# The state space layer's token pieces, tap matrices and value half in a new order

## The chip, the cores and the metric

The kernel runs on one core of one Trainium2 chip. Its time is the device time of one execution in microseconds (us); less is better. The times shown here are of three executions, and of one more that the hardware profiler recorded.

The core has five engines that run side by side and wait for each other through semaphores: PE (TensorE, matrix products), DVE (VectorE), ACT (ScalarE), POOL (GpSimd) and SP (SyncE, which here does nothing but issue transfers). In a profile PEld is the loading of PE's stationary operand. SP, ACT and POOL each have a queue of transfers, shown as SPq, ACTq and POOLq. Each engine takes its instructions in a fixed order, and issuing a transfer is one of them: an engine that has to wait before it may issue does nothing else meanwhile.

## The reference

A trunk of four residual layers on 256 tokens of 1024 channels. Each layer has a token mixer, cross-attention to 256 memory tokens, and a gated MLP. The mixer of layer 2 is a state space layer (S5), and only this layer is changed:

```python
def s5_mixer(h, a_re, a_im, log_dt, b_re, b_im, c_re, c_im, d, w_glu):
    ...                                     # a_bar, b_bar, c_mat: complex, 64 groups of 16 channels, 64 states each
    def chunk_step(state, u_blk):
        bu = jnp.einsum('bcgi,gpi->bcgp', u_blk.astype(jnp.complex64), b_bar)
        a_seq = jnp.broadcast_to(a_bar, bu.shape)
        _, xs = lax.associative_scan(_lin_rec_combine, (a_seq, bu), axis=1)
        xs = xs + a_pow[None] * state[:, None]
        y = jnp.real(jnp.einsum('bcgp,gip->bcgi', xs, c_mat))
        return xs[:, -1], y
    ...
    y = ys.transpose(1, 0, 2, 3, 4).reshape(B, S, D) + d.astype(f32) * u
    y = jax.nn.gelu(y).astype(h.dtype)
    val, gate = jnp.split(y @ w_glu, 2, axis=-1)
    return val * jax.nn.sigmoid(gate)
```

The input `h` of the mixer is the residual stream after an RMS norm. After the mixer the same layer computes the cross-attention, whose keys and values come from the memory tokens alone: `kv = mem_n @ wkv`.

## The kernel before

All weights are fp32. A weight tile of 1 MB is loaded into one of three buffers of the pool `raw`, split into a high and a low part (`whi` by ACT at line 70, `wlo` by DVE or POOL at line 71), and each product is three matmuls (`mm3`, lines 65 to 67). The pool `acts` has two buffers for each of the tags `ah` and `al`, `big` has one (`xs`), and `kv` holds single tiles (`vh`, `vl` and others).

**The state space layer** works on blocks of 8 tokens, 32 of them. Inside a block the output is a product with a matrix of taps; across blocks 64 x 64 complex states are carried. The matrices were made in the layers before and lie in DRAM: `blD` (B, four tiles of 1 MB, `bl`), `tD` (taps, four tiles `tu`) and `caD` (C times powers, four tiles `ou`). In the order of the program the layer does this:

- `rstd` and the scaled tokens `u`, for two halves `tt` of 128 tokens. Each half is written in two column halves, one by DVE and one by ACT (line 962).
- Eight transfers from `u` to `uc` (line 968), 128 KB each, SBUF to SBUF: for each `tt` and each quarter `q` of the channels, 128 pieces of 1 KB go to 16 partitions, those from `32 * q + 16 * tt` on. Quarters 0 and 1 are issued by SP, 2 and 3 by ACT.
- `db`, the product of the skip gain D and the norm's gain, broadcast to 128 partitions by eight small transfers (line 980); POOL multiplies them and then makes the table `tab8` of powers.
- `ur`, a copy of `uc` in another order (line 994, ACT and DVE by turns), transposed by PE into `v` (line 998), then the products with the four `bl` tiles, giving S (line 1012), S transposed into `SX` (lines 1027 and 1029), and the scan, 44 DVE instructions (lines 1049 to 1066) that give the states X. The scan keeps two PSUM banks, `sc` and `two`.
- The products of `v` with the four tap tiles `tu` into the accumulators (line 1078), then of X with the four `ou` tiles (`carry`, line 1098), gelu (lines 1107 and 1109), transposes of the result (line 1115, split at lines 1118 and 1119) and the GLU product with `w_glu`, eight tiles of 1 MB.

**Work between these steps.** PE would idle in this chain, so units of the keys and values of the cross-attention are put at named points by `fill`: `k1 k2` at "u", `k3` at "s" after the products with `bl`, `v0` (the values' first half) at "scan0" and `v1` (the second half) at "scan1". The values' weights `v0`, `v1` are split by POOL.

**What sets the order.** A scheduler orders the instructions of each engine at build time by its own estimates; `behind(x)` makes the following ones come after x in it. A tile's buffer is given to the next tile when the last reader is done, and the transfer that fills it waits for that. The transfers of SP and ACT use eight completion semaphores by turns (DMAHW0 to DMAHW7); a transfer is not issued before the one eight earlier, which had the same semaphore, has landed. The fourth transfer on ACT's queue shares its semaphore with the `bl` tile that SP issues at 814.03 us:

```order
L968 DMA uc_8468<-u_8467 16x8x256 [waits DMAHW2_49,PE_49,Activation_49]
L968 DMA uc_8468<-u_8467 16x8x256 [waits DMAHW4_49]
L968 DMA uc_8468<-u_8467 16x8x256 [waits DMAHW6_49,Activation_49]
L968 DMA uc_8468<-u_8467 16x8x256 [waits DMAHW0_49]
L70 CAST kh_6196<-mm_8516 128x512 [waits PE_49]
```

These are rows of ACT's order before; the last one is the first cast that stands behind the four transfers on ACT.

Of the kernel before, what the change touches and what calls it, by code (L numbers as in the profile page):

```python
# [8 lines left out]
F32 = mybir.dt.float32  # L9
# [5 lines left out]
P = 128  # L15
# [21 lines left out]
class Trunk:  # L37
# [901 lines left out]
    def s5_mixer(self, l, sp):  # L939
        nc, a = self.nc, self.a  # L940
        bls = []

        def land(mm):
            pool, tag = ((self.kv, "vh"), (self.kv, "vl"), (sp, "X"), (self.raw, "raw"))[mm]
            bl = pool.tile([P, 2, 4, 2, 2, 64], F32, tag=tag, name="bl")
            nc.sync.dma_start(bl[:].rearrange("p m q x r k -> p m (q x r k)"), self.blD[:, 2 * mm : 2 * mm + 2, :])
            bls.append(bl)

        land(0)
        land(1)  # L950
        rs = []
        for tt in range(TT):
            rs.append(self.rstd(self.ss[tt]))
        self.fill("u0")
        u = self.big.tile([P, TT, D], F32, tag="xs", name="u")
        uc = sp.tile([P, 8, 16, 16], F32, name="uc")
        chain, firsts, last = [], [None, None], None
        for tt in range(TT):
            r = rs[tt]
            for nh, f in enumerate((nc.vector.tensor_scalar_mul, nc.scalar.mul)):  # L960
                s = slice(512 * nh, 512 * (nh + 1))
                done = f(u[:, tt, s], self.h[:, tt, s], r[:, 0:1])
                firsts = firsts[1:] + [done.ins]

                for q in (2 * nh, 2 * nh + 1):
                    at = 32 * q + 16 * tt
                    queue = nc.scalar if nh else nc.sync
                    moved = queue.dma_start(  # L968
                        uc[at : at + 16].rearrange("c t a j -> c t (a j)"), u[:, tt, 256 * q : 256 * (q + 1)]
                    )  # L970
                    last = last if nh else moved
        chain.append(done.ins)

        chain.append(self.scaled)
        with self.behind(last.ins):
            land(2)
        db = sp.tile([P, 2, 256], F32, name="db")
        for i, row in enumerate((a["s5_d"][0], a["mix_norm_g"][l])):
            for q in range(4):
                nc.sync.dma_start(db[32 * q : 32 * q + 32, i, :], row[256 * q : 256 * (q + 1)].partition_broadcast(32))  # L980
        with self.behind(self.powed):
            nc.gpsimd.tensor_mul(db[:, 0, :], db[:, 0, :], db[:, 1, :])
            tab8 = self.s5_eighths(sp)
# [3 lines left out]
        self.after = [chain, chain + [last.ins]]  # L987
        self.fill("u1")
        self.late = ()
        v = self.acts.tile([P, 16, P], F32, tag="ah", name="v")  # L990
        ev = [nc.scalar.copy, nc.vector.tensor_copy]
        ur = self.acts.tile([P, 16, 8, 16], F32, tag="ah", name="ur")
        for b in range(4):
            ev[b % 2](ur[:, 4 * b : 4 * b + 4], uc[:, ::-1, 4 * b : 4 * b + 4, :].rearrange("p t a j -> p a t j"))
        for b in range(4):
# [8 lines left out]
        for mm in range(4):  # L1004
# [10 lines left out]
                        )  # L1015
            ev[mm % 2](S[:, 2 * mm : 2 * mm + 2].rearrange("p a x b -> p (a x b)"), ps[:])
        self.fill("s")

        SX = self.acts.tile([P, NCH, 2, GP], F32, tag="al", name="SX")
        sv = SX[:].rearrange("p c x (q m) -> p m x q c", m=8)  # L1020
        for b in range(4):
            ps = self.bank()
            for m2 in range(2):
                m = 2 * b + m2
# [3 lines left out]
            for m2 in range(2):  # L1028
                last = ev[1 - m2](sv[:, 2 * b + m2], ps[:, 256 * m2 : 256 * (m2 + 1)].rearrange("p (x q c) -> p x q c", x=2, q=4))
# [36 lines left out]
                steps.append(vec.tensor_add(new, new, pr).ins)  # L1066
        self.late = steps[7:8]
        self.fill("scan0")
        values = self.multiplied

        Y = self.accs()
        for mm in range(4):
            tu = self.raw.tile([P, 2, 2, 4, P], F32, tag="raw", name="tu")
            landed = nc.sync.dma_start(tu[:].rearrange("p r m q k -> p r (m q) k"), self.tD[mm]).ins
            with self.behind(values):
                for m, par, q in [(m, par, q) for m in (2 * mm, 2 * mm + 1) for par in range(2) for q in range(4)]:
                    c0 = (m % 4) * P
                    nc.tensor.matmul(
                        Y[2 * par + m // 4][32 * q : 32 * q + 32, c0 : c0 + P], v[:, 2 * m + par, 32 * q : 32 * q + 32], tu[:, par, m % 2, q, :],
                        start=m % 4 == 0, stop=False, tile_position=(0, 32 * q), skip_group_check=True,  # L1080
                    )
        self.late = steps[-1:]
        self.fill("scan1")
        self.late = ()

        def carry(mm):
            pool, tag = ((self.big, "xs"), (self.acts, "ah"), (self.raw, "raw"), (self.raw, "raw"))[mm]
            ou = pool.tile([P, 2, 4, 2, P], F32, tag=tag, name="ou")
            with self.behind(landed):
                nc.sync.dma_start(ou[:].rearrange("p m q x k -> p m (q x) k"), self.caD[:, 2 * mm : 2 * mm + 2])  # L1090
            for m2 in range(2):
                m = 2 * mm + m2
                for x in range(2):
                    for q in range(4):
                        for par in range(2):
                            rows = slice(64 * par, 64 * par + 64)
                            c0 = (m % 4) * P
                            done = nc.tensor.matmul(
                                Y[2 * par + m // 4][32 * q : 32 * q + 32, c0 : c0 + P], X[rows, x, 8 * q + m, :], ou[rows, m2, q, x, :],
                                start=False, stop=x == 1, tile_position=(64 * par, 32 * q), skip_group_check=True,  # L1100
                            )
            return done.ins
# [8 lines left out]
        def turn(h, yh):  # L1111
# [8 lines left out]
            return last  # L1120

        carry(0)
        carry(1)
        y0, g0 = gelu(0)
        yT = self.act_pair()
        carry(2)
        done = carry(3)
        with self.behind(done):
# [3 lines left out]
        for nh in range(2):  # L1132
            acc = self.accs() if nh else [self.bank() for _ in range(4)]
            for kh in range(2):
                for gate in (1, 0):
# [3 lines left out]
                    for tt in range(TT):  # L1139
                        for k in range(4):  # L1140
                            c = 2 * k + kh
# [5 lines left out]
            for tt in range(TT):  # L1147
# [4 lines left out]
                last = vec.tensor_add(hs, hs, sg)  # L1152
# [271 lines left out]
```

## Time and profile before

| | us |
|---|---|
| median of three executions | 1514.38 |
| lowest and highest | 1512.39, 1520.98 |
| profiled execution, its own time | 1520.19 |
| span from its first to its last instruction | 1518.5 |
| PE busy | 1440.2 (95% of the span) |
| mean granted TensorE clock | 0.974 |

The profiled execution is near the upper end of the three. 1.7 us lie around its span. In rows of the trace times are in us from the start of the span, `out<-in` names the tiles that an instruction writes and reads, and the bracket at a row's end says how long the engine idled before it and what ended that. The layer's mixer lies between 810 and 950 us.

### The profile page before, as it was taken

The page shows a single profiled execution, that of the slowest core. Times are in us where ns is not written, and L with a number is a line of the kernel's source. Part 1 is how long each engine was busy: PE and PEld are TensorE (multiplying, and loading weights), DVE is VectorE, ACT ScalarE, POOL GpSimd, SP SyncE. Part 2 cuts the span into 40 slices and gives each one's busy share as a digit, 9 for nine tenths or more (in the row PEclk, how much of TensorE's full clock was granted, in tenths as well). Part 3 has the DMA queues.
Part 4 walks back from the last instruction along what each step waited for, and adds up shares of the span by engine and source line. Part 5 has one row for each costly group of instructions (what it writes and reads, how often), then busy time and mean ns, then how long its engine had stood idle before and what let it go on. Part 6 is the DMA issues. An engine that isn't in the chain of part 4 may idle for free.

```text
span 1518.5 us, 25333 instructions
## 1 busy us (share of the span) xinstructions
PE 1440.2 (95%) x10318; PEld 1324.3 (87%) x10318; DVE 1096.0 (72%) x1720; ACT 833.4 (55%) x1338; POOL 139.6 (9%) x148
## 2 busy tenths in 40 slices
PE   7999998899899999999997779999999999999997
PEld 7898997798898998999986667989999999899996
DVE  6868677678787666998874755768777686677775
ACT  6554543465677455655544334656555575465553
POOL 3401000000000000011113420000000030000000
PEclk9999999999899999999998889999999999999999
DMA  7567898655543555676577575536564455365551
GB/s 251 202 182 222 230 260 226 203 169 177 156 139 112 165 182 175 226 240 224 194 245 214 206 266 180 181 111 222 187 202 167 155 196 190 113 224 190 169 192 43
DMA packets 211737, 288.10 MB, mean 190 GB/s; under 512 B 26340, under 2 KB 167268, under 8 KB 209700
## 3 DMA queue, kind: packets, MB, share of 16 engines
q1 hardware_dynamic: 198820, 261.74, 52.5%
q0 software_dynamic: 10496, 23.43, 5.8%
q10 hardware_dynamic: 2304, 1.31, 0.4%
q8 instruction: 81, 1.33, 0.4%
q14 instruction: 36, 0.29, 0.1%
HBM read 271.81 MB, written 17.73 MB: 191 GB/s over the span
## 4 chain that ended last, share of the span: by engine, by line
PE 77%; DVE 10%; DMA 8%; issue 2%; ACT 2%; ACTq 0%; SPq 0%; POOL 0%; DVEq 0%; POOLq 0%
PE u L65 9%; PE u L66 9%; PE u L67 9%; PE mm L65 7%; PE acc L67 7%; PE acc L66 7%; PE mm L66 7%; PE acc L65 7%; PE mm L67 7%; DMA raw<-in_ffn_w_up_dram 4%; DVE wlo L71 3%; DVE ug L1253 1%; DMA raw<-in_xa_wkv_dram 1%; PE z L551 1%; DMA blD<-s5o 1%
## 5 line engine op out<-in xcount | busy, mean ns | idle before, releaser
L71 DVE TENSOR_TENSOR wlo<-raw,whi 128x1024 fp32r<-128x1024 f32 x428 | 517.8, 1221 | 181.0 <-ACT whi L70 163.0
L70 ACT CAST whi<-raw 128x1024 fp32r<-128x1024 f32 (+1 forms) x450 | 458.7, 1045 | 231.1 <-DMA raw<-in_ffn_w_up_dram 99.4
L65 PE MATMUL u<-ah,whi 128*128 128x256 f32 x1408 | 400.2, 284 | 2.9 <-DVE ug L1253 2.2
L67 PE MATMUL u<-ah,wlo 128*128 128x256 f32 x1408 | 399.8, 284 | 1.4 <-DVE wlo L71 1.4
L66 PE MATMUL u<-al,whi 128*128 128x256 f32 x1408 | 399.8, 284 | 0.2 <-DVE al L71 0.2
L65 PEld LDWEIGHTS u<-ah,whi 128*128 128x128 f32 x1408 | 271.2, 193 | 7.9 <-issue 3.6
L66 PEld LDWEIGHTS u<-al,whi 128*128 128x128 f32 x1408 | 271.2, 193 | 3.4 <-DVE al L71 0.7
L67 PEld LDWEIGHTS u<-ah,wlo 128*128 128x128 f32 x1408 | 271.1, 193 | 2.0 <-DVE wlo L71 2.0
L1253 DVE SCALAR_TENSOR_TENSOR ug<-u,cwT,ug 128x255 f32<-128x255 f32 x352 | 168.1, 480 | 86.4 <-ACT ug L1251 81.8
L1251 ACT ACTIVATE ug<-u,cwT 128x256 f32<-128x256 f32 x176 | 99.0, 563 | 159.4 <-PE u L67 86.6
L65 PE MATMUL acc<-whi,gg 128*128 128x512 f32 x352 | 140.0, 398 | 11.2 <-ACT gg L70 11.0
L66 PE MATMUL acc<-wlo,gg 128*128 128x512 f32 x352 | 139.5, 396 | 0.0
L67 PE MATMUL acc<-whi,gg 128*128 128x512 f32 x352 | 138.6, 395 | 0.7 <-DVE gg L71 0.6
L66 PE MATMUL mm<-al,whi 128*128 128x256 f32 x384 | 110.0, 287 | 0.1
L65 PE MATMUL mm<-ah,whi 128*128 128x256 f32 x384 | 110.1, 287 | 0.0
L67 PE MATMUL mm<-ah,wlo 128*128 128x256 f32 x384 | 109.7, 286 | 0.0
L176 POOL TENSOR_TENSOR r<-v,mhalf 128x1 f32<-128x1 f32 x28 | 21.0, 751 | 842.0 <-DVE v L172 673.0
L65 PEld LDWEIGHTS acc<-whi,gg 128*128 128x128 f32 x352 | 67.2, 191 | 23.9 <-ACT gg L70 12.2
L67 PEld LDWEIGHTS acc<-whi,gg 128*128 128x128 f32 x352 | 67.0, 190 | 17.2 <-DVE gg L71 2.7
L66 PEld LDWEIGHTS acc<-wlo,gg 128*128 128x128 f32 x352 | 67.3, 191 | 11.0
L66 PEld LDWEIGHTS mm<-al,whi 128*128 128x128 f32 x384 | 74.8, 195 | 0.8 <-DVE al L71 0.6
L65 PEld LDWEIGHTS mm<-ah,whi 128*128 128x128 f32 x384 | 75.0, 195 | 0.1
(354 smaller groups left out, 2605.0 us busy)
## 6 DMA issues: line engine op xcount, KB each, us to landing
raw<-in_ffn_w_up_dram SPq DMA_DIRECT2D x88, 1024.0 KB
raw<-in_ffn_w_down_dram SPq DMA_DIRECT2D x44, 1024.0 KB
raw<-in_xa_wkv_dram SPq DMA_DIRECT2D x30, 1024.0 KB
raw<-in_xa_wq_dram SPq DMA_DIRECT2D x16, 1024.0 KB
raw<-in_xa_wo_dram SPq DMA_DIRECT2D x16, 1024.0 KB
raw<-in_sb_w_qkv_dram SPq DMA_DIRECT2D x12, 1024.0 KB
raw<-in_s_w_glu_dram SPq DMA_DIRECT2D x8, 1024.0 KB
raw<-in_sb_w_o_dram SPq DMA_DIRECT2D x4, 1024.0 KB
```

The costliest lines, as they stand in the source:

```text
L65: mm(out, lh, rh, start=start, stop=False)
L66: mm(out, lh, rl, start=False, stop=False)
L67: self.multiplied = mm(out, ll, rh, start=False, stop=stop).ins
L70: x = self.nc.scalar.copy(hi, src)
L71: y = (eng or self.nc.vector).tensor_sub(lo, src, hi.bitcast(F32))
L176: self.powed = nc.gpsimd.tensor_tensor(r[:], v[:], self.mhalf[:], ALU.pow).ins
L551: mm(out, qk[a][rows, 4 + qc, ks], qk[b][rows, qc, :], start=kt == 1 and n == 0, stop=False, skip_group_check=True)
L1251: nc.scalar.activation(u[:, s, :], out, AF.Identity, bias=cw[3], scale=cw[2])
L1253: nc.vector.scalar_tensor_tensor(u[:, s, sh:], out[:, : T - sh], cw[2 - sh], u[:, s, sh:], ALU.mult, ALU.add)
```

## The change

- All eight transfers of the tokens go to SP's queue. They stand ahead of `db` and of the second and third `bl` tile; the first and fourth `bl` tile are still loaded ahead of them.
- `db` is filled by two transfers with a repeating source in place of eight.
- The four tap tiles: the first goes into a buffer of the tag `ah` and is loaded after the point "s"; the other three stay in `raw`. Its products stand ahead of the second half of the values (`fill("scan1")`), the loads and products of the other three behind it. Before, all four stood ahead of it.
- The `ou` tiles: the second and third now use `raw`, the fourth the buffer `ah` that the first tap tile had.
- `v` and `ur`, which both have the tag `ah`, are made in the other order.

The arithmetic is the same.

```diff
         land(0)
-        land(1)
...
-                for q in (2 * nh, 2 * nh + 1):
-                    at = 32 * q + 16 * tt
-                    queue = nc.scalar if nh else nc.sync
-                    moved = queue.dma_start(
-                        uc[at : at + 16].rearrange("c t a j -> c t (a j)"), u[:, tt, 256 * q : 256 * (q + 1)]
-                    )
-                    last = last if nh else moved
+            for q in range(4):
+                at = 32 * q + 16 * tt
+                last = nc.sync.dma_start(
+                    uc[at : at + 16].rearrange("c t a j -> c t (a j)"), u[:, tt, 256 * q : 256 * (q + 1)]
+                )
         chain.append(done.ins)
 
         chain.append(self.scaled)
+        db = sp.tile([P, 2, 256], F32, name="db")
         with self.behind(last.ins):
+            for i, row in enumerate((a["s5_d"][0], a["mix_norm_g"][l])):
+                nc.sync.dma_start(db[:, i, :], bass.AP(tensor=row.tensor, offset=row.offset, ap=[[256, 4], [0, 32], [1, 256]]))
+            land(1)
             land(2)
-        db = sp.tile([P, 2, 256], F32, name="db")
-        for i, row in enumerate((a["s5_d"][0], a["mix_norm_g"][l])):
-            for q in range(4):
-                nc.sync.dma_start(db[32 * q : 32 * q + 32, i, :], row[256 * q : 256 * (q + 1)].partition_broadcast(32))
...
-        v = self.acts.tile([P, 16, P], F32, tag="ah", name="v")
         ev = [nc.scalar.copy, nc.vector.tensor_copy]
         ur = self.acts.tile([P, 16, 8, 16], F32, tag="ah", name="ur")
+        v = self.acts.tile([P, 16, P], F32, tag="ah", name="v")
...
         self.fill("s")
+        def taps_land(mm):
+            pool, tag = ((self.acts, "ah"), (self.raw, "raw"), (self.raw, "raw"), (self.raw, "raw"))[mm]
+            tu = pool.tile([P, 2, 2, 4, P], F32, tag=tag, name="tu")
+            tus.append(tu)
+            return nc.sync.dma_start(tu[:].rearrange("p r m q k -> p r (m q) k"), self.tD[mm]).ins
+
+        taps_land(0)
...
         self.late = steps[-1:]
+        taps_u(0)
         self.fill("scan1")
         self.late = ()
+        for mm in (1, 2, 3):
+            landed = taps_land(mm)
+            taps_u(mm)
 
         def carry(mm):
-            pool, tag = ((self.big, "xs"), (self.acts, "ah"), (self.raw, "raw"), (self.raw, "raw"))[mm]
+            pool, tag = ((self.big, "xs"), (self.raw, "raw"), (self.raw, "raw"), (self.acts, "ah"))[mm]
```

Two places show what the scheduler makes of it. First SP, from the loads of `bl` to those of `ou` (`raw` from `in_xa_wkv` are weights of the keys and values). Before:

```order
L946 DMA bl<-blD 128x2048 x2
L88 DMA raw<-in_xa_wkv_dram 128x8x256
L980 DMA db<-in_s_d_dram 32x256 x4
L980 DMA db<-in_mix_norm_g_dram 32x256 x4
L946 DMA bl<-blD 128x2048
L968 DMA uc<-u 16x8x256 x4
L946 DMA bl<-blD 128x2048
L88 DMA raw<-in_xa_wkv_dram 128x4x512 x2
L1074 DMA tu<-tD 128x2048 x4
L88 DMA raw<-in_xa_wkv_dram 128x4x512 x2
L1090 DMA ou<-caD 128x2048 x4
```

And now:

```order
L946 DMA bl<-blD 128x2048
L88 DMA raw<-in_xa_wkv_dram 128x8x256
L946 DMA bl<-blD 128x2048
L967 DMA uc<-u 16x8x256 x8
L976 DMA db<-in_s_d_dram 128x1x256
L976 DMA db<-in_mix_norm_g_dram 128x1x256
L946 DMA bl<-blD 128x2048 x2
L88 DMA raw<-in_xa_wkv_dram 128x4x512 x2
L1022 DMA tu<-tD 128x2048
L88 DMA raw<-in_xa_wkv_dram 128x4x512 x2
L1022 DMA tu<-tD 128x2048 x3
L1100 DMA ou<-caD 128x2048 x4
```

The `bl` tile that stood between `db` and `uc` is now issued ahead of all tokens, and three tap tiles stand behind the last two weight tiles of the values, where they stood ahead of them.

Second DVE, at the end of the scan; `vl` is the low part of the values, split out of the PSUM bank in which a half of them was summed. Before:

```order
L1060 COPY sc<-X 128x64
L1064 TENSOR_TENSOR two<-sc,tab_8493 128x64x7
L1066 TENSOR_TENSOR X<-X,two 128x64x7
L1064 TENSOR_TENSOR two<-sc,tab_8493 128x64x7
L1066 TENSOR_TENSOR X<-X,two 128x64x7
L71 TENSOR_TENSOR vl<-mm,vh 128x512 x4
```

And now:

```order
L1067 COPY sc<-X 128x64
L1071 TENSOR_TENSOR two<-sc,tab_8487 128x512
L71 TENSOR_TENSOR vl<-mm,vh 128x512
L1073 TENSOR_TENSOR X<-X,two 128x64x8
L1071 TENSOR_TENSOR two<-sc,tab_8487 128x512
L71 TENSOR_TENSOR vl<-mm,vh 128x512
L1073 TENSOR_TENSOR X<-X,two 128x64x8
L1067 COPY sc<-X 128x64
L1071 TENSOR_TENSOR two<-sc,tab_8487 128x64x7
```

The splits of the first half of the values came after the scan's last step; two of them now stand inside the scan, eight and six of the scan's instructions ahead of its end. The first matmul of `v1`, which took the bank `sc` before and so waited for the last reading of it (line 1064), now takes a bank of `v0` and waits for the first of these splits.

More of the change, by code (lines that the diff above doesn't have):

```diff
@@ L956, in s5_mixer @@
         uc = sp.tile([P, 8, 16, 16], F32, name="uc")
-        chain, firsts, last = [], [None, None], None
+        chain, firsts = [], []
         for tt in range(TT):
             r = rs[tt]
+            firsts = []
             for nh, f in enumerate((nc.vector.tensor_scalar_mul, nc.scalar.mul)):
@@ L962, in s5_mixer @@
                 done = f(u[:, tt, s], self.h[:, tt, s], r[:, 0:1])
-                firsts = firsts[1:] + [done.ins]
-                for q in (2 * nh, 2 * nh + 1):
-                    at = 32 * q + 16 * tt
-                    queue = nc.scalar if nh else nc.sync
-                    moved = queue.dma_start(
-                        uc[at : at + 16].rearrange("c t a j -> c t (a j)"), u[:, tt, 256 * q : 256 * (q + 1)]
-                    )
-                    last = last if nh else moved
+                firsts.append(done.ins)
+            for q in range(4):
[3 more added lines that the diff above has]
+                )
         chain.append(done.ins)
         chain.append(self.scaled)
+        db = sp.tile([P, 2, 256], F32, name="db")
         with self.behind(last.ins):
+            for i, row in enumerate((a["s5_d"][0], a["mix_norm_g"][l])):
+                nc.sync.dma_start(db[:, i, :], bass.AP(tensor=row.tensor, offset=row.offset, ap=[[256, 4], [0, 32], [1, 256]]))
+            land(1)
             land(2)
-        db = sp.tile([P, 2, 256], F32, name="db")
-        for i, row in enumerate((a["s5_d"][0], a["mix_norm_g"][l])):
-            for q in range(4):
-                nc.sync.dma_start(db[32 * q : 32 * q + 32, i, :], row[256 * q : 256 * (q + 1)].partition_broadcast(32))
         with self.behind(self.powed):
@@ L1017, in s5_mixer @@
         self.fill("s")
+        tus = []
+        def taps_land(mm):
[4 more added lines that the diff above has]
+        taps_land(0)
         SX = self.acts.tile([P, NCH, 2, GP], F32, tag="al", name="SX")
@@ L1068, in s5_mixer, with taps_u @@
         self.fill("scan0")
-        values = self.multiplied
         Y = self.accs()
[L1072 to L1075, printed above, removed]
+        def taps_u(mm):
+            with self.behind(self.multiplied):
                 for m, par, q in [(m, par, q) for m in (2 * mm, 2 * mm + 1) for par in range(2) for q in range(4)]:
@@ L1078, in s5_mixer @@
                     nc.tensor.matmul(
-                        Y[2 * par + m // 4][32 * q : 32 * q + 32, c0 : c0 + P], v[:, 2 * m + par, 32 * q : 32 * q + 32], tu[:, par, m % 2, q, :],
+                        Y[2 * par + m // 4][32 * q : 32 * q + 32, c0 : c0 + P], v[:, 2 * m + par, 32 * q : 32 * q + 32], tus[mm][:, par, m % 2, q, :],
                         start=m % 4 == 0, stop=False, tile_position=(0, 32 * q), skip_group_check=True,
```

## The prediction

> **What bounds the kernel now.** The page has PE busy for 95% of the span, so what this change can be worth lies in PE's idle time inside layer 2's mixer. The diff alters the order there and nowhere else. I therefore read PE's waits between 815 and 905 us first (engine, line, what it waited for; us in total, times, longest):
>
> ```profile
> PE mm L998 <- ACT ur L994: 9.9, 1, 9.9
> PE mm L65 <- DVE two L1064: 7.4, 1, 7.4
> PE acc L1078 <- DMA tu<-tD: 3.3, 1, 3.3
> PE acc L1098 <- issue: 3.1, 1, 3.1
> ```
>
> These four are 23.7 us, 1.6% of the kernel. The change aims at the first three. The first stands ahead of the token transposes, and the chain of waits from 812 to 832 us says what ends it:
>
> ```profile
> 814.03 8.38 DMA bl<-blD
> ...
> 822.43 8.41 DMA uc<-u
> ```
>
> A B tile that SP issued at 814.03 took 8.38 us to land, and only then did the last token transfer start. The timeline of ACT shows why:
>
> ```profile
> 813.35 9.65 ACTq L968 DMA_DIRECT2D uc<-u  x4
> 823.04 1.07 ACT L70 CAST kh<-mm 128x512 fp32r<-128x512 f32 x2 [9.11 <-DMA bl<-blD]
> 824.00 2.00 ACT L70 CAST whi<-raw 128x1024 fp32r<-128x1024 f32 x2
> 830.87 1.14 ACT L994 COPY ur<-uc 128x512 f32<-128x512 f32 x2 [4.87 <-DMA uc<-u]
> ```
>
> ACT's fourth issue waits for the semaphore that this B tile holds, so issuing four transfers takes 9.65 us, and the last tokens land at 830.85 (822.43 + 8.41). PE had been through with k2 since 821.66. The timeline of PE, with the start of the scan on DVE and two of its late steps below it, gives the rest:
>
> ```profile
> 831.54 3.67 PE L998 MATMUL mm<-ident,ur 128*128 128x128 f32 x16 [9.88 <-ACT ur L994]
> ...
> 861.62 2.83 PE L1078 MATMUL acc<-tu,v 128*32 128x128 f32 x96
> 867.71 1.93 PE L1078 MATMUL acc<-tu,v 128*32 128x128 f32 x32 [3.26 <-DMA tu<-tD]
> 877.02 1.36 PE L65 MATMUL mm<-whi,mgh 128*128 128x512 f32 x2 [7.38 <-DVE two L1064]
> ...
> 889.86 3.52 PE L1098 MATMUL acc<-ou,X 64*32 64x128 f32 x236
> ...
> 899.83 0.80 PE L65 MATMUL mm<-whi,ah 128*128 128x512 f32 x1 [1.31 <-ACT ah L1118]
> ```
>
> ```profile
> 849.08 1.02 DVE L1049 COPY X<-SX 128x256 f32<-128x256 f32 x1 [0.69 <-ACT SX L1029]
> ...
> 871.70 0.70 DVE L1064 TENSOR_TENSOR two<-sc,tab 128x512 f32<-128x512 f32 x1
> 872.44 0.69 DVE L1066 TENSOR_TENSOR X<-X,two 128x512 f32<-128x512 f32 x1
> ```
>
> I count the back half from the start of the scan, 849.08: v1 starts at +27.94, carry at +40.78, the GLU product at +50.75. The wait at 861 to 877 is not a loss of its own size: the scan runs through it on DVE, and carry needs the scan.
>
> **The front half.** All eight token transfers now stand on SP, ahead of the B tile that held the semaphore, and ACT issues none. SP's price for one is in its timeline:
>
> ```profile
> 814.78 3.22 SPq L968 DMA_DIRECT2D uc<-u  x4
> ```
>
> 0.8 us each. The first half of u was ready for ACT at 813.35, so eight issues end at about 813.2 + 8 x 0.8 = 819.6. Had each landed at once, PE would restart by ACT's own work: its last cast of k2 ends 0.55 after 821.66, two whi casts take 2.00, ur 0.6: **824.9**, a gain of 6.6. That is the best case of this half.
>
> What the transfers themselves take has no row for one queue alone. The windows (us, busy time of PE, PEld, DVE, ACT, POOL, clock, DMA share, GB/s) give the nearest:
>
> ```profile
> 820.00:825.00 5.00, 1.66 (x14) 1.46 (x13) 1.29 (x2) 1.96 (x4) 4.87 (x8) 1.00 1.23 133
> 825.00:830.00 5.00, 0.00 (x0) 0.00 (x0) 0.00 (x0) 1.00 (x2) 0.00 (x0) 0.60 0.98 319
> 830.00:835.00 5.00, 3.46 (x16) 3.21 (x16) 3.63 (x5) 2.31 (x4) 0.96 (x1) 0.50 0.88 326
> ...
> 875.00:880.00 5.00, 2.98 (x7) 2.21 (x8) 3.63 (x6) 0.14 (x1) 5.00 (x3) 0.50 1.01 421
> ```
>
> From 820 to 825, mostly tokens from both queues, the DMA engines are fully busy at 133 GB/s; from 875 to 880, with large tiles, they move 421. So 1 KB token pieces are slow whichever queue holds them, and eight of 128 KB (1.05 MB) take 7.9 us at 133 GB/s. A tile of 1 MB needs 4.95 us from issue to use (the first row of the next fence, 862.76, to 867.71), 2.5 of which are streaming at 421 GB/s; 2.4 are the start. Tokens then flow from 813.2 + 2.4 = 815.6 to 823.5. One more transfer falls among them: POOL's spread of the taps into tD.
>
> ```profile
> 816.02 0.74 POOL L982 TENSOR_TENSOR db<-db 128x256 f32<-128x256 f32 x1 [2.91 <-PE mm L67]
> ...
> 820.98 2.67 POOL L922 DMA_DIRECT2D tD<-kD  x2
> ```
>
> POOL idles 2.91 us ahead of the product of `db`. With `db` behind the tokens, its table comes first, and the spread is issued some 3 us earlier, at 818. I charge half of its 2.5 us of streaming to the tokens: 824.7. With ur (0.63) and the step to PE, PE restarts at **825.4**: a gap of 3.7 in place of 9.88, **6.1 gained**. At half the rate the tokens would land at 831.4 and the gain be −0.6; those are the bounds. I take the value near the top because the 133 GB/s was measured on the same pieces.
>
> [...]
>
> The second and third B tiles now wait behind the tokens in SP's order: landing 2.5 us apart after 824.7, the last at 829.7. PE asks for it after sixteen transposes (3.67) and two tiles of products, at about 831.2. It has 1.5 us to spare; if that is gone, each late us costs one. `db` in two transfers, the swapped buffers of v and ur, and the first tap tile (loaded after the transposes, not needed for over 25 us) cost nothing: what follows them in SP's order has that time as cover.
>
> **The back half.** One tap tile (2.83 / 3 = 0.95) now stands ahead of v1, the other three behind it. v1 waits for the first split of v0, which DVE does inside the scan, after the step of 871.70. It ends near 872.44 + 0.68 = 873.12, so v1 starts at +24.05 in place of +27.94. It takes 12.85 (877.02 to 889.86), then three tap tiles at 0.95: carry starts at **+39.75, 1.1 earlier**. The two splits make the scan 1.3 longer, to about +29.7; this is hidden under v1. So of the 7.4 and 3.3 only 1.1 comes out: taps that had filled the scan now follow it.
>
> A new wait takes this back. The second and third `ou` tiles and the first GLU weight need `raw` buffers that the last three taps now hold until PE has used them, at +37.9, +38.9 and +39.85. SP's rows before:
>
> ```profile
> 862.76 0.32 SPq L1074 DMA_DIRECT2D tu<-tD  x1
> 863.64 1.26 SPq L88 DMA_DIRECT2D raw<-in_xa_wkv_dram  x2
> 865.00 11.55 SPq L1090 DMA_DIRECT2D ou<-caD  x4
> 880.89 0.38 SPq L88 DMA_DIRECT2D raw<-in_s_w_glu_dram  x1
> ```
>
> The first GLU weight was issued at +31.8, 19 us ahead of its use. Now three tiles queue: the first lands 4.95 after +37.95, at +42.9, the others 2.5 apart, at +45.4 and +47.9. On ACT its casts stand ahead of those of the transposed output:
>
> ```profile
> 894.22 1.98 ACT L70 CAST whi<-raw 128x1024 fp32r<-128x1024 f32 x2
> 897.78 2.00 ACT L1118 CAST ah<-yt 128x512 fp32r<-128x512 f32 x2 [1.59 <-PE yt L1115]
> ```
>
> So: +47.9, 1.98, 2.00, start of GLU at **+51.95** in place of +50.75. The back half **loses 1.2**: 1.1 gained and 2.3 given back. Bounds: +49.65, a gain of 1.1, if the weight is in time, and +57 if the tiles don't overlap.
>
> **Sum.** −6.1 + 1.2 = −4.9. The profiled execution took 1520.19, so it would take 1515.3; it lies 5.8 above the median of the runs shown. Against that median, 1514.38 − 4.9: **1510**.
>
> **Rivals.**
>
> *Everything pays.* PE restarts at 824.9 (6.6), carry's 1.1 stays, and the shorter gap ends the half clock: the sixteen transposes run at 0.50, so up to 1.8 of their 3.67 goes, and something of what follows. 8 to 10 gained, about **1506**. For it: the clock is 1.00 at 820 to 825 and falls only in the gap. Against: the gap is still over 3 us, and the weight's +47.9 needs no bad luck.
>
> [...]
>
> *Tiles don't overlap.* `ou`, `ou` and the weight at 4.95 each: landed at +52.8, GLU at +56.8. 6.0 lost against 6.1 gained: **1514.5**. For it: each waits for its own buffer. Against: the three issues are only 1 us apart.
>
> *Slower: the single queue starves.* The two queues made 133 GB/s together; if one carries half, 66, the tokens take 15.8 us and PE restarts at 832.1, 0.55 later than now. With the 1.2 behind, 1.75 lost, up to 3 with the spread: **1516 to 1517**. The point from which it decides is 74 GB/s (14.1 us, landing 829.7). For it: two queues at once were used before. Against: the DMA share was full with both.
>
> **How the numbers follow.** A measurement here tells 0.5%, 7.6 us, from no change. Forecast 1510: 0.45; everything pays, 1506: 0.20; one queue slower, 1512: 0.15; no overlap, 1514.5: 0.10; starved, 1516 to 1517: 0.10. Faster by over 0.5% (under 1506.8) is most of the first rival and a small tail of the forecast: 0.23. Slower needs over 1522: 0.04, from a starved queue and late B tiles together. The range, 1503 to 1518, takes in the lower end of the first rival and the slow one.
>
> **What would show it.** In the changed profile: the gap ahead of L996 (3.7 forecast; over 5 says the queue, under 3.3 the first rival), ended by uc's landing, with no ACT wait for a B tile; v1 starting at +24 after a split on DVE; carry at +39.75; a new wait ahead of the GLU product, ended by its first weight. It is wrong if the gap stays near 10, if B tiles stop PE behind the transposes, or if carry waits for `ou`.

## The result

The changed kernel is **slower**: 1525.07 us against 1516.65 us (medians of seven runs each), a ratio of 1.0062 with a 95% interval of 1.0046 to 1.0079, so 7 to 12 us. The forecast was 1510, its range 1503 to 1518. The profiled execution took 1524.83 us.

PE's waits between 815 and 905 us in the profile after (engine, line, what it waited for; us in total, times, longest) answer to the first view of the prediction:

```profile
PE mm L65 <- DVE vl L71: 11.5, 1, 11.5
PE mm L1010 <- DMA bl<-blD: 5.3, 2, 3.8
PE mm L996 <- ACT ur L992: 4.6, 1, 4.6
PE acc L1108 <- DMA ou<-caD: 4.5, 2, 3.2
PE mm L65 <- ACT ah L1128: 1.7, 1, 1.7
```

The 9.9 us for the tokens became 4.6. Two waits are new: 5.3 for the second and third B tile, 4.5 for two `ou` tiles. The 11.5 us ahead of v1 stand where 7.4 and 3.3 stood; they are no loss of their own size, since the scan runs through them. The timeline of PE around the B tiles, and the first piece that the chain of waits from 808 to 840 us gives for them:

```profile
824.05 3.29 PE L996 MATMUL mm<-ident,ur 128*128 128x128 f32 x16 [4.64 <-ACT ur L992]
827.28 1.08 PE L1010 MATMUL mm<-bl,v 128*32 128x128 f32 x32
832.18 1.08 PE L1010 MATMUL mm<-bl,v 128*32 128x128 f32 x32 [3.82 <-DMA bl<-blD]
```

```profile
818.34 16.25 DMA bl<-blD
```

A B tile that is issued at 818.34 lands 16.25 us later; the one in the chain before took 8.38, and a tap tile 4.95. SP's timeline shows what stands ahead of it:

```profile
810.91 5.21 SPq L967 DMA_DIRECT2D uc<-u  x8
816.44 0.62 SPq L976 DMA_DIRECT2D db<-in_s_d_dram  x1
817.12 0.59 SPq L976 DMA_DIRECT2D db<-in_mix_norm_g_dram  x1
817.75 1.02 SPq L946 DMA_DIRECT2D bl<-blD  x2
```

Behind the scan, the timelines of PE, with the scan's start on DVE above it, and of ACT:

```profile
849.01 0.43 DVE L1056 COPY X<-SX 128x256 f32<-128x256 f32 x1 [0.67 <-ACT SX L1036]
...
872.48 0.80 PE L65 MATMUL mm<-whi,mgh 128*128 128x512 f32 x1 [11.49 <-DVE vl L71]
...
886.17 2.83 PE L1083 MATMUL acc<-tu,v 128*32 128x128 f32 x96
888.92 1.16 PE L1108 MATMUL acc<-ou,X 64*32 64x128 f32 x64
893.28 1.16 PE L1108 MATMUL acc<-ou,X 64*32 64x128 f32 x64 [3.20 <-DMA ou<-caD]
895.79 3.04 PE L1108 MATMUL acc<-ou,X 64*32 64x128 f32 x108 [1.35 <-DMA ou<-caD]
...
902.60 0.50 PE L65 MATMUL mm<-whi,ah 128*128 128x512 f32 x1 [1.65 <-ACT ah L1128]
```

```profile
895.80 1.06 ACT L1119 ACTIVATE uc<-uc 128x1024 f32<-128x1024 f32 x1 [8.94 <-DVE uc L1117]
898.51 1.99 ACT L70 CAST whi<-raw 128x1024 fp32r<-128x1024 f32 x2 [1.66 <-DMA raw<-in_s_w_glu_dram]
900.54 2.00 ACT L1128 CAST ah<-yt 128x512 fp32r<-128x512 f32 x2
```

Taps 1 to 3 end v1's stretch, then carry waits twice for `ou`, and ACT waits for the first GLU weight. A later wait, inside the GLU (PE's waits from 905 to 925), is new too; before, only the wait for `ah` stood there:

```profile
PE acc L65 <- ACT whi L70: 2.0, 1, 2.0
PE mm L65 <- ACT ah L1128: 1.5, 1, 1.5
```

For all comparisons I cut the mixer at four marks: the first ACT row of `u`; the first row of the scan on DVE; the first carry and first GLU matmul; and the first transpose of the cross-attention on PE, where the mixer ends. In us, worked out from the timelines; the ratio is to the kernel before. One profiled execution, that of the first kernel with two queues below, had a granted clock of 0.75 and took 1760.55 us, so it has no row here and serves only for the spacing of its transfers and for what waited for what.

| kernel | u to scan | scan to carry | scan to GLU | scan to end | mixer | ratio of times |
|---|---|---|---|---|---|---|
| before | 36.5 | 40.8 | 50.8 | 99.2 | 135.7 | 1 |
| before, again | 35.1 | 41.7 | 50.3 | 98.2 | 133.2 | 0.9994 [0.9975, 1.0012] |
| the change | 38.7 | 39.9 | 53.6 | 103.9 | 142.6 | 1.0062 [1.0046, 1.0079] |
| front alone | 38.5 | 37.8 | 46.6 | 93.6 | 132.1 | 1.0025 [1.0009, 1.0041] |
| front alone, again | 37.2 | 39.3 | 48.4 | 95.2 | 132.4 | 0.9995 [0.9976, 1.0014] |
| back alone | 37.4 | 44.4 | 58.8 | 108.7 | 146.1 | 1.0081 [1.0065, 1.0096] |
| db behind B | 34.3 | 41.0 | 55.7 | 105.5 | 139.8 | 1.0041 [1.0024, 1.0058] |
| db in eight | 36.0 | 36.3 | 50.0 | 99.8 | 135.8 | 1.0007 [0.9988, 1.0026] |
| db in two, alone | 35.1 | 40.5 | 49.5 | 97.8 | 132.9 | 1.0009 [0.9986, 1.0032] |
| taps ahead | 37.6 | 36.9 | 49.6 | 98.0 | 135.6 | 1.0026 [1.0004, 1.0048] |
| front mended | 33.7 | 40.2 | 51.1 | 99.7 | 133.4 | 0.9960 [0.9941, 0.9978] |
| all mended | 32.4 | 35.9 | 44.4 | 90.6 | 123.0 | 0.9948 [0.9928, 0.9968] |

In the two profiles the change lost 2.2 us ahead of the scan and 4.7 behind it, 6.9 in all, which is the lower end of the measured 7 to 12; against the second profile of the kernel before, it lost 9.4.

The 2.2 are more than the two waits: 5.2 were gained at the tokens and 5.3 lost at the B tiles. The other 2.1 lie in products that ran longer. The last 64 products with B took 3.64 us, with a granted clock of 0.50 from 835 to 840 us, where all 128 took 4.15 in the kernel before; from the transposes to the end of these products the change took 1.2 us more, the waits left out. From there to the scan it took another 0.9 us more.

### The profile page after: what moved, and what is told of

Its sections match the earlier page's. It is cut to its first block, busy times and chain, and to the rows that moved or that the text cites. A ratio compares the mean times of both kernels' runs of the same rounds, so it can differ in the third digit from the quotient of the medians.

```text
span 1523.1 us, 25325 instructions
## 1 busy us (share of the span) xinstructions
PE 1439.6 (95%) x10318; PEld 1324.5 (87%) x10318; DVE 1095.1 (72%) x1720; ACT 832.7 (55%) x1338; POOL 140.6 (9%) x148
## 4 chain that ended last, share of the span: by engine, by line
PE 67%; DVE 13%; DMA 12%; ACT 3%; issue 3%; SPq 1%; ACTq 0%; POOL 0%; DVEq 0%; POOLq 0%
DMA raw<-in_ffn_w_up_dram 8%; PE mm L66 7%; PE mm L65 7%; PE mm L67 7%; PE u L66 7%; PE u L65 7%; PE u L67 7%; PE acc L67 6%; PE acc L66 6%; PE acc L65 6%; DVE wlo L71 4%; DVE ug L1263 2%; ACT whi L70 2%; DMA bl<-blD 1%; PE z L551 1%
```

## The experiments

### How far a difference can be trusted

The kernel before, unchanged, as a kernel of its own.

> The kernel before, unchanged, as a measure of what a difference means: its ratio should be 1.000 within 0.3%, and a second profile shows how far the span up to u, the mixer (135.7 us from u to the first transpose of the cross-attention) and the rest vary between executions. If the mixer varies by 3 us or more, single profiles cannot carry the differences read so far.

Measured: 0.9994, interval 0.9975 to 1.0012. The mixer took 133.2 us in place of 135.7, in good part because its tokens landed 2.1 us earlier. So one profile's mixer is good to some 2.5 us, and smaller differences are read below only where a named wait accounts for them.

### The two halves apart

The token half alone: the change's lines from `land(0)` to the copy of `v`, with taps, values and `ou` of before.

```diff
-        taps_land(0)
...
-        taps_u(0)
+        for mm in range(4):
+            tu = self.raw.tile([P, 2, 2, 4, P], F32, tag="raw", name="tu")
...
         self.fill("scan1")
-        for mm in (1, 2, 3):
-            landed = taps_land(mm)
-            taps_u(mm)
```

(This diff and the next are against the changed kernel.)

> The token half of the change alone: uc on SP, db in two transfers, the later B tiles behind them; taps and values in the order of before. The trace of the changed kernel puts the start of the scan 2.2 us later, counted from u, than before: 5.2 gained at the wait for the tokens, 6.6 lost from the transposes to k3, 0.8 in k3 and the turn of S. If the two halves do not depend on each other, this kernel is 2 us slower than before (+1 to +3), with 5 us of PE waits for the B tiles. If the tap half caused part of the B tiles' lateness (its first tap tile is loaded right behind them), those waits shrink and it is 2 to 5 us faster.

> The token half alone once more, since its first look contradicts itself: its profile had the mixer 2 to 3.5 us shorter than the two profiles of before, its times were 3.8 us longer; the rest of that profile was 7 us longer in places where both kernels have the same instructions. If those 7 us were one execution's chance, a second profile shows u near 812 us and a time near 1516 to 1519 beside it, and the ratio falls towards 1.000. If they belong to this build, u is again near 817 and the ratio stays at 1.002 to 1.004.

Measured: 1.0025 and, again, 0.9995; the two intervals only just overlap, so such an interval may be somewhat too narrow. The first profile reached `u` at 817.5 us, the second at 812.1, in layers whose instructions are the same: that part was chance. The half alone makes no difference that can be told. As expected, the path to the scan is as long as in the change (38.5 and 37.2); PE's waits in the first of the two profiles hold the same pair of gains and losses:

```profile
PE acc L1076 <- DMA tu<-tD: 4.7, 1, 4.7
PE mm L996 <- ACT ur L992: 4.7, 1, 4.7
PE mm L65 <- DVE vl L71: 4.2, 2, 3.1
PE mm L1010 <- DMA bl<-blD: 4.0, 2, 2.6
```

The third row is new. With the taps in the order of before, v1 now waits for a split of v0 and no longer for the scan's last reading of `sc`: it got another PSUM bank. It started 23.5 us after the scan's start (24.6 in the second profile, behind a cast of ACT) in place of 27.9, which is most of what that half is shorter behind the scan.

The tap half alone: lines from the point "s" to `carry` as changed, with tokens, `db` and B tiles of before.

```diff
+        land(1)
...
-            for q in range(4):
-                at = 32 * q + 16 * tt
-                last = nc.sync.dma_start(
+                for q in (2 * nh, 2 * nh + 1):
+                    at = 32 * q + 16 * tt
+                    queue = nc.scalar if nh else nc.sync
...
-            land(1)
```

> The tap half of the change alone: the first tap tile in ah ahead of the values' second half, the other three behind it; tokens, db and B tiles as before. By the changed kernel's trace this half costs 2.9 us from the start of the scan to the first GLU product and 1.9 more inside the GLU, where its weights come late: 4.7 us slower than before (+3.5 to +6). My forecast on record had 1.2 slower. If the lateness of the ou tiles and GLU weights came from the front (tap tiles shifted by the late B tiles), it is within 1.5 us of before.

Measured: 1.0081, 10 to 15 us slower, over twice the expected. PE's waits say why:

```profile
PE mm L65 <- DVE two L1073: 16.0, 1, 16.0
PE mm L998 <- ACT ur L994: 6.5, 1, 6.5
PE acc L1110 <- DMA ou<-caD: 4.9, 2, 3.5
```

Here v1 took a bank of the scan and waited 16.0 us for its last use; it started 28.0 after the scan's start, where before had it (27.94), and three taps, `ou` and the weights came behind that. So the early start of v1, the one gain that I gave the tap half, hangs on which bank the scheduler hands out, and without the token half it handed out another. The halves don't add.

### What made the B tiles late

`db` behind the B tiles:

```diff
         with self.behind(last.ins):
-            for i, row in enumerate((a["s5_d"][0], a["mix_norm_g"][l])):
-                nc.sync.dma_start(db[:, i, :], bass.AP(...))
             land(1)
             land(2)
+            for i, row in enumerate((a["s5_d"][0], a["mix_norm_g"][l])):
+                nc.sync.dma_start(db[:, i, :], bass.AP(...))
```

> The changed kernel with the two db transfers behind the second and third B tile in place of ahead of them. Theory: the two repeating transfers run on few of the 16 DMA engines, and the parts of every later tile on those engines come about 4 us late; then the B tiles now land near 826 and 829 us, PE's waits for them fall from 5.3 us to 1 or less, and the kernel is 4 us faster than the change. Rival: the B tiles are late because they queue behind slow token pieces and beside the spread of the taps; then the waits stay at 4 to 5 us and the time moves by less than 1.5.

Measured: u to scan 34.3 us in place of 38.7, PE's wait for B 1.1:

```profile
PE mm L1010 <- DMA bl<-blD: 1.1, 1, 1.1
```

The time went from 1.0062 to 1.0041, some 3 us; these two intervals overlap, so it is PE's wait that tells. The trace has each moment at which a transfer's semaphore rises: sixteen for a tile. The profile counts 16 DMA engines, so I take each of these entries for one engine that is done with its share; this is an estimate, since the trace names no engine. For the second B tile, in us after `u` begins, sorted:

```
the change   16.54 16.54 16.57 16.58 16.59 16.63 16.71 16.78 16.82 16.83 17.00 17.75 | 21.11 21.23 21.57 21.71
db behind B  14.42 14.43 14.45 14.50 14.52 14.56 14.60 14.66 14.68 14.69 14.70 14.70   14.72 14.75 14.75 15.41
db itself (first row, the change)            7.20 | 14.01 14.04 14.99 15.30
```

In the change twelve entries are there by 17.75 and four come 3.4 to 4.0 us later; the third B tile and the weight tile behind it show the same twelve and four, with gaps of 1.6 to 2.2 and 1.2 to 1.8. Each of the two `db` transfers makes five entries: one about a microsecond after its issue, and four late ones. Each of the eight `db` transfers of the kernel before makes sixteen, which come within 0.9 us. Without `db` ahead the four entries of the B tile come with the others. So, by that estimate, `db` in two transfers ran on four of sixteen engines, by its shape 32 pieces of 1 KB on each, twice, and the tiles issued behind it had to wait for these four. Its source pattern begins with a dimension of 4, as many as there are late entries; whether the one sets the other, and what the lone early entry is, no run here shows.

The four late entries are not the whole delay. The third B tile was complete 24.2 us after `u` began in the change and 19.4 with `db` behind it. 2.2 of these 4.8 us are the gap ahead of the four; the other 2.6 came on the other twelve as well. With `db` ahead of it the tile was issued 1.5 us later, and it landed behind the first spread of the taps into `tD`; with `db` behind it, it landed ahead of that.

`db` in eight transfers, in the changed place:

```diff
-                nc.sync.dma_start(db[:, i, :], bass.AP(...))
+                for q in range(4):
+                    nc.sync.dma_start(db[32 * q : 32 * q + 32, i, :], row[256 * q : 256 * (q + 1)].partition_broadcast(32))
```

> The changed kernel with db in eight small broadcasts again, in the changed place (behind the tokens). Each of them has to wait for the semaphore of a token transfer, so the B tiles are issued only after the last tokens landed, near 824. Theory (two repeating transfers clog a few DMA engines): B lands near 829 and 831.5, PE waits 2 to 3 us in place of 5.3, and the kernel is 2 to 3 us faster than the change in spite of the later issue. Rival (order behind the tokens): B lands no earlier than in the change, 832 and 834.6 or later, and the time is the same or up to 2 us longer.

Measured: 1.0007, 8 us faster than the change where 2 to 3 were expected. The front gained these 2 to 3 (u to scan 36.0), though the B waits, 3.9 us, were longer than expected, since B is issued only at 826.6, 12.9 us after `u` begins. All sixteen entries of the third B tile now lie between 21.0 and 22.6: it was issued 5.4 us later than in the change and complete 1.6 us earlier. The other 4 us are behind the scan, where nothing was edited: in this build the first split of v0 stands ahead of the scan's last loop (its three rounds of block carries), and v1 starts 19.8 us after the scan's start in place of 23.5:

```profile
868.72 0.68 DVE L71 TENSOR_TENSOR vl<-mm,vh 128x512 fp32r<-128x512 f32 x1
869.32 0.26 DVE L1068 COPY sc<-X 128x64 f32<-128x64 f32 x1
```

Again an order that the scheduler chose.

`db` in two transfers, alone in the kernel before:

```diff
-            for q in range(4):
-                nc.sync.dma_start(db[32 * q : 32 * q + 32, i, :], row[256 * q : 256 * (q + 1)].partition_broadcast(32))
+            nc.sync.dma_start(db[:, i, :], bass.AP(...))
```

> The kernel before with one line of the change: db in two transfers with a repeating source in place of eight, in its old place ahead of the third B tile and the tokens. Theory: the two transfers run on 5 of the 16 DMA engines and hold up on those engines all that stands behind them: the B tile of 1 MB and each token transfer are complete on the first engines 4 us or more before the last, the tokens land 3 to 6 us later than before (18.3 us after u begins) and the kernel is 2 to 6 us slower. Rival: two transfers in place of eight only save SP 2.4 us of issuing; tokens land at the same time or earlier and the time is 0 to 2 us shorter.

Measured: 1.0009, no difference, and the tokens landed 15.6 us after `u` begins, not later than before (18.3 and 16.2). That is a miss. (The five engines expected were the five entries; one of them is the early one.) The B tile behind `db` does show twelve entries by 6.0 and four at 8.2 to 8.6, but SP was through with `db` so much sooner that this tile was issued 2.5 us earlier, and it was complete at 8.6 in place of 9.8. What the four late entries cost thus depends on what else is queued, and when.

### What sets the pace of the tokens

Quarters 0 and 1 on SP, 2 and 3 on ACT (first kernel), or 0 and 2 on SP, 1 and 3 on ACT (second, with `q % 2 == 1` in the diff's first new line):

```diff
-                last = nc.sync.dma_start(
+                on_act = q >= 2
+                moved = (nc.scalar if on_act else nc.sync).dma_start(
...
+                last = last if on_act else moved
```

> The changed kernel with the tokens on two queues as before (quarters 0 and 1 on SP, 2 and 3 on ACT) and all else in its order. In the change the eight pieces landed one by one, 1.2 us apart (131 KB in 1.2 us: 109 GB/s), the last 12.9 us after u begins. [...] Theory of the DMA engines: small packets fill the 16 engines whichever queue holds them, and the last lands near 12 to 13 us again. The stall for the B tiles stays or grows.

> [...] If a queue has a rate of its own (two queues are twice as fast): the same as the other run on two queues, near 8.5 us.

Measured, the eight landings in us after `u` begins:

```
one queue (the change)        4.00  5.27  6.43  7.65  8.84 10.07 11.28 12.94
two queues                    3.99  5.10  6.26  7.31  8.45  9.61 10.68 11.56
two queues, 0 and 2 on SP     3.97  5.22  7.08  7.64  8.83 10.06 11.26 12.92
```

The seven gaps between landings average 1.28 us with one queue, 1.08 with two, and 1.28 with two when SP has quarters 0 and 2; up to the seventh piece they average 1.21, 1.12 and 1.22, which for 131 KB are 108, 118 and 108 GB/s. A second queue does not double the pace: the rival on starved queues is dead, and of the hope that two would be faster at most 1.4 us are left (11.56 against 12.94), in one profile. The window of the change's profile says the same (columns as in the prediction):

```profile
815.00:820.00 5.00, 4.41 (x37) 4.21 (x36) 0.01 (x1) 0.55 (x2) 3.35 (x4) 1.00 1.17 110
```

With the tokens on one queue this row has 110 GB/s at a DMA share of 1.17. Two queues were not nearly twice as fast, and their pieces landed one after another. What sets this pace, and why the two ways of sharing out the quarters differ (1.12 and 1.22), stays open: a transfer of the same pieces to more partitions was not tried.

The first of the two kernels took 1.0092 (1.0061 to 1.0122), the second, in its only execution, 1528.31 us; both profiles show v1 waiting for the scan's bank (12.7 and 15.5 us), as the back half alone did.

### What made `ou` and the GLU weights late

Only the products of taps 1 to 3 are moved, ahead of v1; their loads stay behind those of v1's weights:

```diff
         taps_u(0)
-        self.fill("scan1")
+        self.fill("scan1w")
         for mm in (1, 2, 3):
             landed = taps_land(mm)
             taps_u(mm)
+        self.fill("scan1")
```

"scan1w" holds the loads of v1's weights alone, "scan1" now only v1.

> The changed kernel with one thing moved: the products of tap tiles 1 to 3 stand ahead of those of v1 (all four tiles ahead, as before), while their loads stay behind the loads of v1's weights as in the change. Theory: the change's loss behind the scan comes from raw buffers that taps 1 to 3 hold until after v1, so that two ou tiles and the first GLU weights are issued 38 us after the scan's start. Here these buffers come free near +19; PE's waits for ou (4.5 us) and for GLU's weight splits (1.7 and 2.0) go, carry starts near +36.6 and GLU near +45 to +46 in place of +53.6; the kernel is 8 to 10 us faster than the change and 1 to 4 faster than before. Rival: carry is set by the scan and by DVE's splits, and GLU by ACT's order; then carry stays at +39 to +40 and at most 3 us come back.

Measured: 1.0026, some 5 us faster than the change but still slower than before. Carry starts at +36.9 as expected, without a wait for `ou`. GLU starts at +49.6, not +45 to +46. ACT's timeline:

```profile
886.55 1.99 ACT L70 CAST whi<-raw 128x1024 fp32r<-128x1024 f32 x2
889.35 1.06 ACT L1120 ACTIVATE uc<-uc 128x1024 f32<-128x1024 f32 x1 [0.81 <-DVE uc L1118]
895.66 1.04 ACT L70 CAST whi<-raw 128x1024 fp32r<-128x1024 f32 x1 [5.26 <-DMA raw<-in_s_w_glu_dram]
896.61 1.98 ACT L1129 CAST ah<-yt 128x512 fp32r<-128x512 f32 x2
```

The first weight is cast early (886.55). But the scheduler now put a cast of the *second* weight ahead of the casts of the transposed output, and ACT stood 5.26 us for its landing; PE waited 6.2 for `ah`. The theory of the held buffers holds, and a new wait took about half of what it returned: by an estimate, without the 4.5 us that this wait is longer than the change's 1.7, the GLU would have started at +45.1.

### All three mended

```diff
+            land(1)
+            land(2)
+            for i, row in enumerate((a["s5_d"][0], a["mix_norm_g"][l])):
+                for q in range(4):
...
+        self.fill("scan1")
...
-            return last
+            return hi, last
```

`db` in eight stands behind the B tiles, v1 behind taps 1 to 3 as in the last run, and `turn` hands back ACT's cast (`hi`) too, so that the second weight's casts stand behind it.

> The changed kernel with the three costs found so far taken out at once: db in eight small transfers behind the second and third B tile (no transfer on few DMA engines, B straight behind the tokens), the products of taps 1 to 3 ahead of v1, and ACT's casts of the transposed output ahead of those of the second GLU weight. Theory: from u to the scan 33 to 34 us (38.7 in the change, 35 to 36.5 before), from the scan to the cross-attention 92 to 94 (103.9 in the change, 98 to 99 before); mixer 126 to 128 us, 14 to 16 us faster than the change and 6 to 9 faster than before. If one of the costs was named wrongly, it shows as a wait of PE of its size: over 2 us for B tiles, over 2 for ou, over 3 ahead of the GLU.

Measured: 1510.59 us, ratio 0.9948 (0.9928 to 0.9968): **5 to 11 us faster than before** and some 17 faster than the change. From u to the scan 32.4 us, from the scan to the end 90.6, both a little under the forecast. PE's waits from 815 to 905 us:

```profile
PE acc L1084 <- DMA tu<-tD: 6.5, 2, 3.9
PE mm L997 <- ACT ur L993: 4.0, 1, 4.0
PE mm L65 <- ACT SX L1037: 1.9, 1, 1.9
PE mm L65 <- ACT ah L1130: 1.6, 1, 1.6
PE acc L1110 <- issue: 1.6, 1, 1.6
PE mm L66 <- POOL wlo L71: 1.2, 1, 1.2
PE mm L1011 <- DMA bl<-blD: 1.0, 1, 1.0
```

None of the three named costs is left at its size: B tiles 1.0, no wait for `ou`, 1.6 ahead of the GLU. What each of the three edits gave in this kernel was not told apart. The 6.5 us for taps lie inside the scan.

With the back of before and only the front mended (B tiles, then `db` in eight):

> The token half alone, taps as before, with db in eight small transfers behind the B tiles in place of two ahead of them. Theory: PE waits 4 to 5 us for the tokens and at most 1 for B tiles; from u to the scan 33 to 34 us. Against the token half alone as in the change (38.5): 4 to 5 us faster, and 2 to 4 faster than before. Rival: the B tiles are late for another reason than db; then u to scan stays above 37.

Measured: 0.9960 (0.9941 to 0.9978), u to scan 33.7, B waits 0.3:

```profile
PE acc L1077 <- DMA tu<-tD: 4.8, 1, 4.8
PE mm L997 <- ACT ur L993: 4.0, 1, 4.0
...
PE mm L1011 <- DMA bl<-blD: 0.3, 1, 0.3
```

So the front path is 3.5 to 4.8 us shorter than with the change's `db`, and 3 to 9 us of time are gained on before, about the 6.1 forecast. That `db` stood in the way of the B tiles is shown by their wait. That all of the gain comes from there is not: the path to the scan is 1.4 to 2.8 us shorter than in the two profiles of before, and the whole mixer, 133.4, is no shorter than in the second (133.2).

## Why the prediction was wrong

- **The first wait.** Right, and nearly right in size. ACT issues nothing and no longer stands behind a B tile. The tokens landed 12.9 us after `u` begins, where the forecast had 12.1 (824.7 less 812.6): the term was 1.05 MB at 133 GB/s, and one queue carried 108. The gap is 4.6 in place of 3.7, the gain 5.2 in place of 6.1. One queue slower than two had a chance of 0.15, at 1512; no run shows the rate behind that time, and what was measured is 108 GB/s with one queue and 118 and 108 with two. The share of the spread, some 1.2 us, was charged too high: in the three runs with `db` behind the B tiles, where the spread lands later, the tokens came only 0.7 us sooner, at 12.3.
- **"`db` in two transfers ... cost nothing".** This step failed, and it cost most. I counted SP's issues and bytes and took what follows in SP's order for cover. The two transfers, with four late entries each where a tile of 1 MB has sixteen, held back what stood behind them. The B tiles were to land by 17.1 us after `u`; the last one came at 24.2. With `db` behind the B tiles (three runs) it comes at 19.4: 4.8 of the 7.1 us are `db`'s place ahead of them, by its four late entries and the later issue; the other 2.3 are the slower tokens and what else was under way. The 1.5 us to spare became a wait of 5.3. I had noted that each late us beyond the spare costs one, and named "if B tiles stop PE behind the transposes" as a sign of being wrong, but I had no rival for it.
- **v1 and carry.** v1 was to start at +24.05 after the scan's start and carry at +39.75; they did at +23.5 and +39.9. That this rests on a PSUM bank was seen (it was in the order of the build), but not that another build of the same back half gives the bank away.
- **"The back half loses 1.2."** The mechanism was right, its size was not. The tiles behind the last taps, two of `ou` and the first GLU weight, landed at +44.2, +46.7 and +49.4, not +42.9, +45.4 and +47.9: the first took 5.9 us from issue to landing, not 4.95, and the rest stayed 2.5 to 2.7 apart. GLU came at +53.6 in place of +51.95, a loss of 2.8 up to there. That carry would wait for `ou` followed from the forecast's own numbers, +42.9 and +45.4 against a start at +39.75, and yet its last paragraph gives it as a sign of being wrong; it waited 4.5 us. The step stopped at the first weight; the later ones use the same three buffers, and PE waited 2.0 more inside the GLU, a loss of 1.9 that no term held. Together 4.7.
- **Sum.** −6.1 + 1.2 was forecast; the profiles show +2.2 + 4.7. In the front 0.9 of the miss are the tokens, 5.3 the B tiles and 2.1 the slower products, for which the forecast had no term; behind the scan it is 3.5. The half clock that the fastest rival hoped to end was back behind the second B wait (0.50 from 835 to 840 us). `db` alone does not account for the sign: with it behind the B tiles the kernel was still slower than before (1.0041), in eight transfers no faster (1.0007), and with the held buffers alone mended slower (1.0026). It was faster with both mended, and ACT's casts with them (0.9948). The slow rival had the right sign with the wrong mechanism, and the chance of slower, 0.04, was far too small: of the edits that I had costed at nothing, one used up the cover that I had given to all of them.

## What to carry to other kernels

Before a transfer is called free, look in a trace at when its last completion entries come as well as at its bytes: here a broadcast in two transfers held up four of the sixteen entries of each large tile queued close behind it, by 3.4 to 4.0 us on the first. When a step moves behind another one, follow its buffers and not only its products: three tap tiles that cost PE 2.8 us cost the kernel 4.7 through the loads that waited for their buffers. And where a scheduler hands out banks and orders, test the halves of a change apart and together, and look at more than one profile; here the same source lines behind the scan took between 99.8 and 109.6 us (the second kernel on two queues).

## What the runs showed of the hardware that I had not expected

- Behind two transfers of 128 KB with four late entries each, four of the sixteen entries of the next 1 MB tile came 3.4 to 4.0 us after the other twelve, and those of the next four tiles 1.2 to 2.2 us after.
- Token pieces of 128 KB land each 1.1 to 1.3 us on average, from one queue or from two.
- The mixer of one unchanged kernel differed by 2.5 us between two profiles, and two sets of executions of another gave ratios of 1.0025 and 0.9995, whose intervals only just overlap.
